# Routing and places of a mixture of experts: one product for all places, reordered rows, plain writes, held weight loads

## The chip, the cores and the metric

The kernel runs on one core of one Trainium2 chip. The metric is the device time of that core in microseconds (us), the median of several runs. Before the change it is 1528.69 us (median of 3 runs, 1525.78 to 1528.85).

## What is computed

Two transformer blocks on 512 tokens of 1024 channels: a recurrent mixer with a feed-forward layer, then a second mixer with a mixture of experts. Only the last part matters here. Shortened:

```python
h2 = rms_norm(x) * g2 * (1 + sc2) + sh2        # 512 rows of 1024
g_idx = argmax(h2 @ w_group + b_group)          # one group of 4 for each token
top_vals, e_idx = top_k(logits of that group's 4 experts, 2)
weights = p_g * softmax(top_vals)
for each of 16 experts:                         # d_expert = 256
    y += (silu(h2 @ gate) * (h2 @ up) * combine) @ down
out = x + gt2 * y
```

Each token goes to two experts, so an expert has 64 tokens on average. The kernel keeps 128 places for each expert and one further slot (number 16) for an expert with more.

## The kernel before, in words

Everything is unrolled. TensorE (PE) multiplies, VectorE (DVE) and ScalarE (ACT) prepare operands and take results out of PSUM, SyncE (SP) issues the plain loads, GpSimd (POOL) issues the DMAs that accumulate, gather or scatter. float32 products are made of three passes on split operands (`hi`, `lo`): ACT copies a weight piece into `hi` (L1279), DVE subtracts it into `lo` (L1280).

The order of the end of the kernel:

- **Last product** (L1282 to L1309). For each of 4 blocks `tb` of 128 tokens, 24 matmuls (L1289 to L1291) give the second half of the output projection. `x2half` (L1253) multiplies by `gt1r`, adds to the rows `x1t` (L1255, L1256) and squares (L1257). Then the block's rows are transposed (L1295), multiplied by the router (L1298), turned back (L1300) and summed into the logits `lg` (L1303 to L1305); the inverse root comes from `rsq1` (L227 to L232). Last, DVE forms the normed row `h` (L1308) and POOL adds it with an accumulating DMA to `d_h2` in DRAM (L1309; the profile calls it `d_h`), which an earlier SP DMA had filled with the shift `sh2`. Here the planner orders the engines' work by priority.
- **Routing** (L1313 to L1339). `largest` (L1315) finds the first and second choice of each token, `abf` marks its two experts, a triangular product (L1336) counts ranks, `cola` is the rank plus one and `col_` the rank.
- **Places.** For an expert, `onehot` (L1342) compares the ranks of all tokens with 0 to 127, giving `O`, and `placed` (L1346) multiplies `O` with `tk` (token number and weight in parts) by 4 matmuls (L1349). `infos` (L1350) takes the token numbers into `idx` and the weights into `wcl` (L1352 to L1355). Expert 0's `idx` is made first and alone (L1451 to L1454), experts 0 to 4 come in `places` (L1356), each later one inside the expert loop, five experts ahead.
- **Gather.** `gather` (L1403) lets POOL fetch the 128 rows of an expert from `d_h2` into `xg` by `idx` (L1405); three buffers. Rows beyond the expert's count are skipped.
- **Expert loop** (from L1477, an order written out by hand for PE, DVE and ACT). An expert's weights are six pieces of 512 KB: 0 to 3 for gate and up, 4 and 5 for down. `up_piece` (L1415 to L1424), `up_end` with the silu (L1426), `act_in` (transposes L1431, copies L1433), `down` (L1436 to L1445) and the scatter, an indirect accumulating DMA into `out` (L1446). PE does expert e+1's first up piece, then e's transposes L1431, then the rest of e+1's up, then e's down. At e=3 to 7 DVE has the steps of `further`, at e=11 those of `extra` (L1383 to L1389), for slot 16.
- **Weight loads.** `wfetch` (L1209) issues a piece on SP (L1215) into the next of 26 slots; a slot is given back when its piece is converted (or, for piece 5, used). Ten pieces (`NR`) are issued before the last branch merge, the others as slots come free. `pieces` (L1394) is the order in which pieces are used, `ensure` converts up to `LA`=3 pieces ahead.

With slot 16 there are 17 experts of 6 pieces, 102 pieces.

## Time and profile before

| | us |
|---|---|
| median of 3 runs | 1528.69 |
| the profiled execution | 1528.76 |
| its span, first to last instruction | 1527.0 |
| PE busy | 1431.6 (94%) |
| DVE busy | 1035.8 (68%) |
| ACT busy | 642.9 (42%) |
| POOL busy | 100.5 (7%) |

The profile has several views. The page gives busy shares, and the span in 40 slices of 38 us, with a digit for the tenths that an engine was busy. Windows give the same for stretches that one chooses, with the granted clock of TensorE as a share of full speed and the share of time in which the 16 DMA engines had packets under way. The timeline lists instructions by their start. The DMA view lists issues with the median time from issue to landing. In the timeline a row is: start, duration, engine, source line, operation, output and inputs, shapes, and in brackets the idle time before it and what ended that.

### The profile page before, as it was taken

Reading aid. Unit: us, or ns where it says so; the run is one execution under the profiler, and the core shown is the slowest. Engines: PE = TensorE matmul, PEld = TensorE weight load, DVE = VectorE, ACT = ScalarE, POOL = GpSimd, SP = SyncE. Lnnn points to the kernel's source line nnn. Section 1 sums busy time; section 2 is a strip of 40 time slices with the busy share of each in tenths; the row PEclk is TensorE's granted clock in tenths of the full one; section 3 lists DMA queues with packets and bytes.
Section 4 is the critical chain, followed back from the end, with each engine's and each line's share of the span. In section 5 each row is a group of like instructions: output and inputs, shape, how many; then the busy total and the mean of one; then the engine's idle time right before and its main releaser. Section 6 shows DMA issues by size and latency. Waiting matters only on the chain. (4 is left out here: it accounts for less than half of the span.)

```text
span 1527.0 us, 23008 instructions
## 1 busy us (share of the span) xinstructions
PE 1431.6 (94%) x8916; PEld 1110.6 (73%) x8916; DVE 1035.8 (68%) x1988; ACT 642.9 (42%) x1042; POOL 100.5 (7%) x116
## 2 busy tenths in 40 slices
PE   7999979899999999899999999999899999399996
PEld 4777857677777787777777777777678887276764
DVE  4887868668787774644649967654543445689994
ACT  5554436233433443323343324463622343265662
POOL 0111100000000000000001000000000000123232
PEclk9999989899999999999999999999899999699998
DMA  5443524052556446554243211122043245889960
GB/s 196 141 142 135 204 65 165 16 177 67 186 198 202 165 141 183 169 203 139 75 151 106 86 62 62 57 99 77 23 179 125 97 149 196 282 295 355 332 219 14
DMA packets 78706, 226.63 MB, mean 148 GB/s; under 512 B 19520, under 2 KB 20160, under 8 KB 78592
## 3 DMA queue, kind: packets, MB, share of 16 engines
q1 hardware_dynamic: 68736, 202.25, 38.4%
...
HBM read 208.52 MB, written 28.07 MB: 155 GB/s over the span
## 5 line engine op out<-in xcount | busy, mean ns | idle before, releaser
L155 DVE TENSOR_TENSOR lo<-raw,hi 128x1024 fp32r<-128x1024 f32 (+1 forms) x183 | 210.7, 1152 | 209.5 <-ACT hi L154 208.4
L154 ACT ACTIVATE hi<-raw 128x1024 fp32r<-128x1024 f32 (+1 forms) x183 | 183.2, 1002 | 389.4 <-PE g L170 223.1
L171 PE MATMUL g<-bh,lo 128*128 128x512 f32 x376 | 152.3, 405 | 2.5 <-DVE lo L155 2.4
L169 PE MATMUL g<-bh,hi 128*128 128x512 f32 x376 | 152.3, 405 | 0.0
L170 PE MATMUL g<-bl,hi 128*128 128x512 f32 x376 | 150.5, 400 | 0.0
L171 PE MATMUL g<-hh,lo 128*128 128x512 f32 x336 | 133.7, 398 | 6.7 <-DVE lo L155 6.7
L169 PE MATMUL g<-hh,hi 128*128 128x512 f32 x336 | 133.7, 398 | 0.0
L170 PE MATMUL g<-hl,hi 128*128 128x512 f32 x336 | 133.2, 397 | 0.0
L171 PEld LDWEIGHTS g<-bh,lo 128*128 128x128 f32 x376 | 71.5, 190 | 22.2 <-DVE lo L155 4.2
L169 PEld LDWEIGHTS g<-bh,hi 128*128 128x128 f32 x376 | 71.8, 191 | 19.1 <-issue 2.0
L170 PEld LDWEIGHTS g<-bl,hi 128*128 128x128 f32 x376 | 71.4, 190 | 16.2 <-issue 0.2
L169 PE MATMUL g<-xh,hi 128*128 128x512 f32 x200 | 80.2, 401 | 0.0
L171 PEld LDWEIGHTS g<-hh,lo 128*128 128x128 f32 x336 | 63.8, 190 | 22.5 <-DVE lo L155 7.6
L861 DVE SCALAR_TENSOR_TENSOR acc<-raw,ca,acc 128x1024 f32<-128x1024 f32 x42 | 53.8, 1282 | 38.7 <-DMA raw<-in_wmod 38.5
L171 PE MATMUL g<-xh,lo 128*128 128x512 f32 x200 | 79.7, 398 | 0.0
L170 PE MATMUL g<-xl,hi 128*128 128x512 f32 x200 | 79.4, 397 | 0.0
L169 PEld LDWEIGHTS g<-hh,hi 128*128 128x128 f32 x336 | 63.9, 190 | 17.9 <-ACT hi L154 3.4
L170 PEld LDWEIGHTS g<-hl,hi 128*128 128x128 f32 x336 | 63.7, 190 | 14.8
L890 DVE SCALAR_TENSOR_TENSOR c<-g,vec,c 128x511 f32<-128x511 f32 x88 | 65.6, 745 | 1.1
L754 PE MATMUL g<-hi,fl 128*128 128x512 f32 x136 | 53.4, 393 | 0.0
L755 PE MATMUL g<-lo,fh 128*128 128x512 f32 x136 | 53.4, 392 | 0.0
L753 PE MATMUL g<-hi,fh 128*128 128x512 f32 x136 | 53.1, 391 | 0.0
...
## 6 DMA issues: line engine op xcount, KB each, us to landing
raw<-in_wexp SPq DMA_DIRECT2D x89, 512.0 KB, 8.4
raw<-in_win SPq DMA_DIRECT2D x74, 512.0 KB, 3.5
raw<-in_wmod SPq DMA_DIRECT2D x48, 512.0 KB, 4.1
raw<-in_wup SPq DMA_DIRECT2D x44, 512.0 KB, 4.1
raw<-in_wdn SPq DMA_DIRECT2D x22, 512.0 KB, 4.0
raw<-in_wout SPq DMA_DIRECT2D x16, 512.0 KB, 4.6
ws<-in_wexp SPq DMA_DIRECT2D x13, 512.0 KB, 10.3
raw<-in_wA SPq DMA_DIRECT2D x12, 512.0 KB, 3.4
```

Of the source, the lines that this page charges most:

```text
L154: S.activation(hi[:,:f],raw[:,:f],AF.Copy)
L155: V.tensor_tensor(lo[:,:f],raw[:,:f],hi.bitcast(F32)[:,:f],op=OP.subtract)
L169: PE.matmul(ps,hi[:,sl],xh[k],start=(k==0),stop=False)
L170: PE.matmul(ps,hi[:,sl],xl[k],start=False,stop=False)
L171: PE.matmul(ps,lo[:,sl],xh[k],start=False,stop=(k==n-1))
L753: PE.matmul(ps,xh[k][:,sl],w[kk][0],start=(k==0),stop=False)
L754: PE.matmul(ps,xl[k][:,sl],w[kk][0],start=False,stop=False)
L755: PE.matmul(ps,xh[k][:,sl],w[kk][1],start=False,stop=(k==2*n-1))
L861: else: V.scalar_tensor_tensor(acc,raw,ca[:,k:k+1],acc,op0=OP.mult,op1=OP.add)
L890: for k in (1,2): V.scalar_tensor_tensor(c[:,k:],ps[:,:512-k],Vc(f'fw{2-k}',i),c[:,k:],op0=OP.mult,op1=OP.add)
```

## The change

Five things are changed. (1) The last product, its logits and the routing get an order written by hand, in which block tb-1's transposes and logits stand between block tb's products. (2) Only blocks 0 and 1 of `d_h2` are filled with the shift and accumulated into; for blocks 2 and 3 the shift is added on DVE and SP writes the rows plainly. (3) The places of all 16 experts are found at once: the rank `rk` of each token's first and second choice gives eight one-hots `Ak` of 128 places, and one product of 8 matmuls gives all 16 columns of `idx`, a second one later all weights; the per-expert `onehot`, `placed` and `infos` go away, except for slot 16. (4) No further weight piece is issued by SP until the first gather has landed: a DMA of 16 numbers that reads the gathered rows (`d_hold`) is put in SP's queue ahead of them. The ten first pieces remain. (5) Expert 15's down product is moved between the second and third up piece of slot 16.

```diff
-    with tc.issue_after(ug_.ins): nc.sync.dma_start(d_h2,bass.AP(tensor=d_mod.tensor,offset=d_mod.offset+3072,ap=[[0,512],[1,1024]]))
-
-    oh=pd2.tile([128,384],F32,name='oh',tag='l'); nc.sync.dma_start(oh,A['oh'])
+
+    oh=pd2.tile([128,384],F32,name='oh',tag='l'); oh_=nc.sync.dma_start(oh,A['oh'])
+    with tc.issue_after(oh_.ins): nc.sync.dma_start(d_h2[0:256,:],bass.AP(tensor=d_mod.tensor,offset=d_mod.offset+3072,ap=[[0,256],[1,1024]]))
...
-    for i in (0,2,3):
+    for i in range(4):
         m=pe_.tile([128,1024],F32,name='modr',tag=f'modr{i}'); modr.append(m)
         nc.sync.dma_start(m,bass.AP(tensor=d_mod.tensor,offset=d_mod.offset+2048+1024*i,ap=[[0,128],[1,1024]]))
-    gt1r,a2r,gt2r=modr
+    gt1r,sh2r,a2r,gt2r=modr
...
+    hold=[None]
     def wnext(whole=False):
         if not AS: AS.extend([act2.tile([128,2,1024],F32 if t_[2]=='1' else FR,name='ws',tag=t_) for t_ in ('Ah0','Al0','Ah1','Al1')])
-        while todo and any(p!='AS' or not todo[0][1] for p,_ in slots): wfetch(*todo.pop(0))
+        if hold[0]:
+            with tc.issue_after(hold[0]) if hold[0]!='done' else ExitStack():
+                while todo and any(p!='AS' or not todo[0][1] for p,_ in slots): wfetch(*todo.pop(0))
+            if len(done)>=3: hold[0]='done'
...
-        x2half(tb,1,ps)
-        nc.scalar.dma_start(out[sl,:],x1t[tb])
...
+    man=ExitStack(); man.enter_context(tc.manual_schedule(engines={ET.PE,ET.DVE,ET.Activation}))
...
-        v=small(3,'nv'); V.tensor_scalar(v[:,0:1],ssq[:,tb,0:1],ssq[:,tb,1:2],1e-6,op0=OP.add,op1=OP.add)
-        rsq1(v[:,0:1],v[:,1:2],v[:,2:3])
...
-        lgi=V.scalar_tensor_tensor(lg[:,tb,:],lg[:,tb,:],v[:,1:2],rbias,op0=OP.mult,op1=OP.add)
-        h=pw.tile([128,1024],F32,name='h2',tag='h2')
-        with tc.issue_after(lgi.ins):
-            V.scalar_tensor_tensor(h,x1t[tb],v[:,1:2],a2r,op0=OP.mult,op1=OP.mult)
-        G.dma_start(d_h2[sl,:],h,accum_op=OP.add)
+        V.scalar_tensor_tensor(lg[:,tb,:],lg[:,tb,:],blk[tb]['v'][:,1:2],rbias,op0=OP.mult,op1=OP.add)
+    def inverse(tb):
+        blk[tb]['v']=v=small(3,'nv'); V.tensor_scalar(v[:,0:1],ssq[:,tb,0:1],ssq[:,tb,1:2],1e-6,op0=OP.add,op1=OP.add)
+        rsq1(v[:,0:1],v[:,1:2],v[:,2:3])
+    def scaled(tb):
+        blk[tb]['h']=h=pw.tile([128,1024],F32,name='h2',tag='h2'); V.tensor_tensor(h,x1t[tb],a2r,op=OP.mult)
+    def rows_out(tb):
+        v=blk[tb]['v'][:,1:2]
+        if tb<2:
+            h=pw.tile([128,1024],F32,name='h2',tag='h2'); V.scalar_tensor_tensor(h,x1t[tb],v,a2r,op0=OP.mult,op1=OP.mult)
+            G.dma_start(d_h2[tb*128:tb*128+128,:],h,accum_op=OP.add)
+        else:
+            h=blk[tb]['h']; V.scalar_tensor_tensor(h,h,v,sh2r,op0=OP.mult,op1=OP.add)
+            nc.sync.dma_start(d_h2[tb*128:tb*128+128,:],h)
+    for tb in range(4):
+        ps=pg.tile([128,512],F32,name='g',tag='g')
+        product(tb,ps,0); product(tb,ps,1)
+        if tb: turned(tb-1)
+        product(tb,ps,2)
+        if tb: logits(tb-1)
+        product(tb,ps,3)
+        if tb: added(tb-1)
+        x2half(tb,1,ps)
+        nc.scalar.dma_start(out[tb*128:tb*128+128,:],x1t[tb])
+        if tb: rows_out(tb-1)
+        inverse(tb)
+        if tb>=2: scaled(tb)
+    turned(3); logits(3); added(3); rows_out(3)
...
-    os_=tt('os',4,4); V.tensor_tensor(os_,o1_,o2_,op=OP.add)
-    abf=pe_.tile([128,4,16],BF,name='abf'); V.tensor_tensor(abf.rearrange('p t (g e) -> p t g e',g=4),os_,g44,op=OP.mult)
+    og=pe_.tile([128,2,4,16],BF,name='og')
+    for k,oh_ in enumerate((oh1,oh2)): V.tensor_tensor(og[:,k].rearrange('p t (g e) -> p t g e',g=4),v4(oh_)[:,:,1:5,:],g44,op=OP.mult)
+    abf=pe_.tile([128,4,16],BF,name='abf'); V.tensor_tensor(abf,og[:,0],og[:,1],op=OP.add)
...
+    og8=og.rearrange('p k t e -> p (k t) e')
+    bt=pe_.tile([128,2,4,2,16],BF,name='bt')
+    for k in range(2): V.tensor_tensor(bt[:,k],og[:,k][:,:,None,:].to_broadcast([128,4,2,16]),tk[:,:,0,0:2][:,:,:,None].to_broadcast([128,4,2,16]),op=OP.mult)
+    ge=tt('ge',4); V.tensor_tensor(ge,lg[:,:,0:4],mx1[:,:,0][:,:,None].to_broadcast([128,4,4]),op=OP.subtract); S.activation(ge,ge,AF.Exp)
     cola=tt('cola',16); V.scalar_tensor_tensor(cola,rps[:,0:64].rearrange('p (t e) -> p t e',t=4),1.0,abf,op0=OP.add,op1=OP.mult)
-    col_=tt('col_',16); V.tensor_scalar(col_,cola,1.0,None,op0=OP.subtract)
-    iota=C3('iota')
+    ck=sq_pool.tile([128,2,4,16],F32,name='ck',tag='sq',bufs=3); V.tensor_tensor(ck,og,cola[:,None].to_broadcast([128,2,4,16]),op=OP.mult)
+    rk=pe_.tile([128,8],F32,name='rk'); V.tensor_reduce(rk,ck.rearrange('p k t e -> p (k t) e'),axis=AX,op=OP.add)
+
+    iota=C3('iota'); iota1=C3('iota1')
+    Ak=pe_.tile([128,8,128],BF,name='Ak')
+    for k in range(2): V.tensor_tensor(Ak[:,4*k:4*k+4],iota1[:,None,:].to_broadcast([128,4,128]),rk[:,4*k:4*k+4][:,:,None].to_broadcast([128,4,128]),op=OP.is_equal)
     idx=pe_.tile([128,17],U32,name='idx'); wcl=pe_.tile([128,17],F32,name='wcl')
+    def at_places(B,n):
+        ps=pt()
+        with order():
+            for i in range(8): PE.matmul(ps[:,:n],Ak[:,i,:],B[:,i,:],start=(i==0),stop=(i==7))
+        return ps
+    ps=at_places(bt.rearrange('p k t c e -> p (k t) (c e)'),32)
+    cnt=pe_.tile([128,16],F32,name='cnt'); V.tensor_copy(cnt,rps[:,64:80])
+    ips=pe_.tile([128,32],F32,name='ips'); V.tensor_copy(ips,ps[:,:32])
+    V.scalar_tensor_tensor(idx[:,0:16],ips[:,0:16],4096.0,ips[:,16:32],op0=OP.add,op1=OP.add)
...
-    def places(e0,e1):
-        ips=pm.tile([128,17,8],F32,name='m',tag='m')
-        for e in range(e0,e1): placed(onehot(col_[:,:,e]),lambda tb:tk[:,tb,e,:],ips,e)
-        infos(ips,e0,e1,wcl,idx)
...
-    pieces+=[(16,4),(16,5)]
+    pieces[-6:]=[(16,0),(16,1),(15,4),(15,5),(16,2),(16,3),(16,4),(16,5)]
...
-    O=onehot(col_[:,:,0]); ips=pm.tile([128,17,8],F32,name='m',tag='m')
-    with order():
-        for i in range(8): PE.matmul(ips[:,0,0:1],O[:,i//2,:],tk[:,i//2,0,i%2:i%2+1],start=(i==0),stop=(i==7))
-    idx0=pe_.tile([128,1],U32,name='idx0'); V.tensor_scalar(idx0,ips[:,0,0:1],4096.0,None,op0=OP.add)
-    xgs=[gather(idx0)]; ensure(2)
-
-    b4=lambda t_: t_[:,:,None].to_broadcast([128,4,4])
-    b44=lambda t_: t_[:,:,None,None].to_broadcast([128,4,4,4])
-    ge=tt('ge',4); V.tensor_tensor(ge,lg[:,:,0:4],b4(mx1[:,:,0]),op=OP.subtract); S.activation(ge,ge,AF.Exp)
+    xgs=[gather(idx[:,i:i+1]) for i in range(3)]
+
+    d_hold=dten('d_hold',[1,16]); hold[0]=nc.sync.dma_start(d_hold,xgs[0][0:1,0:16]).ins
+    ensure(1)
...
+    xin=rows_in(xgs[0],0); ps=psum()
...
-    places(0,5); xgs.append(gather(idx[:,1:2]))
+        V.tensor_copy(wp[:,p],m12)
+        if p<2: V.tensor_tensor(m12,m12,wp[:,p],op=OP.subtract)
+    bw=pe_.tile([128,8,3,16],BF,name='bw')
+    for p in range(3): V.tensor_tensor(bw[:,:,p,:],og8,wp[:,p].rearrange('p k t -> p (k t)')[:,:,None].to_broadcast([128,8,16]),op=OP.mult)
+    for p in range(4):
+        up_piece(ps,xin,p,piece(0,p))
+        if p==1: wps=at_places(bw.rearrange('p i c e -> p i (c e)'),48)
+    wpc=pe_.tile([128,48],F32,name='wpc'); V.tensor_copy(wpc,wps[:,:48])
+    V.tensor_tensor(wcl[:,0:16],wpc[:,0:16],wpc[:,16:32],op=OP.add); V.tensor_tensor(wcl[:,0:16],wcl[:,0:16],wpc[:,32:48],op=OP.add)
+    a=up_end(ps,wcl[:,0:1])
+    xin=rows_in(xgs[1],1); xgs.append(gather(idx[:,3:4]))
+    for p in range(3): V.tensor_tensor(tk[:,:,:,2+p],bw[:,0:4,p,:],bw[:,4:8,p,:],op=OP.add)
...
+    for e in range(17):
+        O=None
+        if e<13: xgs.append(gather(idx[:,e+4:e+5]))
+        if e==3: fur=further()
+        if 3<=e<8: next(fur,None)
+        if e==11: xps=pm.tile([128,17,8],F32,name='m',tag='m'); O=extra(0,xps,16)
+        if e==8:
+            e0=nc.values_load(ei[0:1,0:1],min_val=0,max_val=15,engines=[ET.SP])
+            w0=[(A['wexp'][bass.ds(e0,1),p].rearrange('o p f -> (o p) f'),p==5) for p in range(6)]
+            todo+=w0[:2]+wx(15,(4,5))+w0[2:]
+        if e<16: ps=psum(); up_piece(ps,xin,0,piece(e+1,0))
+        aa=act_in(a)
+        if e<16:
+            for p in range(1,4):
+                if e==15 and p==2: down(aa,piece(e,4),piece(e,5),idx[:,e:e+1])
+                up_piece(ps,xin,p,piece(e+1,p))
+            a=up_end(ps,wcl[:,e+1:e+2])
+        if O: placed(*O)
+        if e<15: xin=rows_in(xgs[e+2],e+2)
+        if e!=15: down(aa,piece(e,4),piece(e,5),idx[:,e:e+1])
+        if O: infos(xps,16,17,wcl,idx)
...
-            if s_<16: ips=pm.tile([128,17,8],F32,name='m',tag='m'); O=(onehot(col_[:,:,s_]),lambda tb:tk[:,tb,s_,:],ips,s_)
...
-            if O: infos(ips,s_,s_+1,wcl,idx)
```

## Rows read from the trace of the kernel before

**Rows 1.** The page: PE's busy tenths in 40 slices of the span.

```profile
PE   7999979899999999899999999999899999399996
```

**Rows 2.** Windows: length, PE, PEld, DVE, ACT, POOL busy, PE clock, DMA share, GB/s.

```profile
1310.00:1320.00 10.00, 2.05 (x31) 1.13 (x31) 7.47 (x25) 0.28 (x1) 0.84 (x1) 0.50 1.03 321
1324.00:1328.00 4.00, 0.00 (x0) 0.00 (x0) 3.69 (x15) 0.00 (x0) 1.60 (x1) 0.50 1.02 418
1350.00:1375.00 25.00, 25.00 (x124) 18.53 (x124) 23.66 (x37) 17.61 (x26) 5.25 (x4) 1.00 0.94 311
1425.00:1450.00 25.00, 25.00 (x118) 18.36 (x117) 24.77 (x43) 17.22 (x27) 6.24 (x4) 1.00 1.01 334
1475.00:1500.00 25.00, 25.00 (x114) 18.75 (x113) 23.02 (x29) 17.62 (x26) 5.67 (x3) 1.00 0.13 26
```

**Rows 3.** Timeline from the last product's end to expert 0's list of rows.

```profile
1305.42 0.40 PE L1291 MATMUL g<-lo,gh 128*128 128x512 f32 x1
...
1307.80 0.69 DVE L1256 TENSOR_TENSOR x1t<-x1t,g 128x512 f32<-128x512 f32 x1
...
1311.63 0.24 DVE L1303 TENSOR_REDUCE l<-m 128x20 f32<-128x80 f32 x1 [0.86 <-PE m L1300]
...
1312.28 1.28 DVE L1308 SCALAR_TENSOR_TENSOR h<-x1t,nv,modr 128x1024 f32<-128x1024 f32 x1
1313.47 0.23 DVE L1316 TENSOR_REDUCE mx<-lg 128x20 f32<-128x80 f32 x1
...
1317.72 0.69 DVE L1344 TENSOR_TENSOR O<-cst,col__11733 128x512 bf16<-128x512 f32 x1
...
1318.89 0.16 DVE L1454 TENSOR_SCALAR idx<-m 128x1 uint32<-128x1 f32 x1 [0.48 <-PE m L1453]
```

**Rows 4.** Timeline: the first gather, and PE's first use of it.

```profile
1323.73 1.87 POOL L1405 DMA_INDIRECT xg<-d_h,idx  x1 [9.03 <-ACT ws L1279]
...
1332.23 0.66 PE L1411 MATMUL m<-cst,xg 128*128 128x128 f32 x2 [3.86 <-DMA xg<-d_h,idx]
```

**Rows 5.** DMA, us to landing: last block's write (1313.86), gathers 1, 2, plain DRAM writes.

```profile
d_h<-h POOLq DMA_DIRECT2D x1, 512.0 KB, 8.9
xg<-d_h,idx POOLq DMA_INDIRECT x1, 8.4
xg<-d_h,idx POOLq DMA_INDIRECT x1, 5.8
d_x<-xr SPq DMA_DIRECT2D x4, 512.0 KB, 2.7
```

**Rows 6.** Timeline: transposes L1431, once for each expert (0, 3, 11, 12, 15).

```profile
1345.67 0.38 PE L1431 MATMUL m<-cst,a 128*128 128x128 f32 x2
...
1375.41 0.38 PE L1431 MATMUL m<-cst,a 128*128 128x128 f32 x2
...
1458.65 0.38 PE L1431 MATMUL m<-cst,a 128*128 128x128 f32 x2
...
1471.27 0.38 PE L1431 MATMUL m<-cst,a 128*128 128x128 f32 x2
...
1500.52 0.38 PE L1431 MATMUL m<-cst,a 128*128 128x128 f32 x2
```

**Rows 7.** DMA, weight pieces issued before 1190, in 1350 to 1375, 1450 to 1475.

```profile
raw<-in_wexp SPq DMA_DIRECT2D x10, 512.0 KB, 5.0
...
raw<-in_wexp SPq DMA_DIRECT2D x13, 512.0 KB, 6.6
...
raw<-in_wexp SPq DMA_DIRECT2D x9, 512.0 KB, 13.7
```

**Rows 8.** Timeline: slot 16's transposes, its last result, its scatter.

```profile
1508.03 0.38 PE L1431 MATMUL m<-cst,a 128*128 128x128 f32 x2
...
1512.45 0.69 DVE L1445 TENSOR_TENSOR ye<-g,modr 128x512 f32<-128x512 f32 x1 [0.86 <-PE g L1444]
...
1515.88 1.54 POOL L1446 DMA_INDIRECT out<-ye,idx  x1 [5.15 <-DMA out<-ye,idx]
```

More of the change, by code (lines that the diff above doesn't have):

```diff
@@ L1294, in build, with product, turned @@
+    blk=[{} for _ in range(4)]
+    def product(tb,ps,p):
+        sl=slice(tb*128,tb*128+128); hi,lo=wl1[p]
+        for kk in range(2):
+            k=2*p+kk; c=slice(kk*512,kk*512+512)
+            PE.matmul(ps,mh[k][:,sl],hi[:,c],start=(k==0),stop=False)
+            PE.matmul(ps,ml[k][:,sl],hi[:,c],start=False,stop=False)
+            PE.matmul(ps,mh[k][:,sl],lo[:,c],start=False,stop=(k==7))
+    def turned(tb):
         ps=pt((128,4,128))
         for k in range(4): PE.transpose(ps[:,k,:],x1t[tb][:,(4+k)*128:(4+k)*128+128],ident)
-        hc=pw.tile([128,4,128],F32,name='hc',tag='hc'); S.activation(hc,ps,AF.Copy)
+        blk[tb]['hc']=hc=pw.tile([128,4,128],F32,name='hc',tag='hc'); S.activation(hc,ps,AF.Copy)
```

75 lines of the change are left out of this document (20 added, 55 removed).

## The prediction, made before the change was run

> **What bounds the kernel now.** I read the page first: PE is busy in nearly every slice, with one dip near the end, at digit 35 of 40 [rows 1]. A slice is 38 us, so the dip lies near 1310. All edits but one small write lie from there on. The windows, read second, show a hole: from 1310 to 1320 PE works 2 of 10 us at a granted clock of 0.50, which is the level of 1.2 GHz, while the DMA engines have packets under way all the time; from 1324 to 1328 PE does nothing and DMA moves 418 GB/s [rows 2]. The timeline tells who is waited for. The last product ends at 1305.8, its rows are complete at 1308.5, the logits bring the routing to 1313.5, expert 0's list is there at 1319.05 [rows 3]. But its gather starts only at 1323.7 and PE only at 1332.2 [rows 4]: the last block's accumulating write, issued at 1313.86, took 8.9 us and landed at 1322.8, and then the gather took 8.4 us [rows 5].
>
> Behind the hole the loop runs with three engines near their limits: from 1425 to 1450 DVE is busy 24.8 of 25 us and the DMA share is 1.01 [rows 2]. L1431 comes once for each expert, so its spacing is the period: (1375.41-1345.67)/3 = 9.91 us, (1458.65-1375.41)/8 = 10.41 while DVE also has the steps of `further`, 12.62 with `extra`, and (1500.52-1471.27)/3 = 9.75 at the end [rows 6], where DVE has fallen to 23.0 of 25 and loads are over [rows 2]. 9.75 is what PE alone needs. The loads are a bound that hides: a piece issued between 1350 and 1375 lands after 6.6 us, one between 1450 and 1475 after 13.7 [rows 7]. The queue grows, so supply is slower than use, and only the lead built up in the hole carries the loop.
>
> **Part by part.**
> *Start of the routing.* In the new order `added(2)` stands ahead of `x2half(3)` on DVE, about 0.6 us, but the planner's former insertion of `h` between L1255 and L1256 (1.28 us as L1308 [rows 3]) goes, so rows are complete some 0.3 us earlier. Then DVE has `rows_out(2)` (1.28), `inverse(3)` (about 1.5, seven small operations) and `scaled(3)` (1.28, like L1308) before the logits' sum, which was reached 3.1 us after the rows [rows 3]; the three end after 3.9. Net +0.4: L1316 at 1313.9. A wait is added here: `scaled(3)` needs the buffer of block 1's row, free when its accumulating DMA lands. That is issued near 1301.8 and I give it the 8.9 us of its kind [rows 5], so 1310.7, just as DVE gets there; a later landing would delay the logits queued behind it on DVE one for one.
>
> *Places.* One more small operation (0.25), two small products and `ge` while PE counts ranks (0.2 not hidden), `ck` and `rk` in place of `col_` (+0.35), a second one-hot operation of 0.69 that starts 0.63 after the first, and one copy (0.2): +1.65 on a path that took 1313.47 to 1319.05 [rows 3]. All lists at 1319.05+0.4+1.65 = 1321.1.
>
> *Rows written plainly.* `rows_out(3)` ends at 1313.9 and SP has nothing else due, so the write is issued then. Plain DRAM writes of this size land after 2.7 us [rows 5], at 1316.6; even 4 us more would be hidden by the places. The gather then waits for the list and starts at 1321.4 rather than 1323.7.
>
> *Gather, loads held.* Its latency was 8.4 us among loads and 5.8 for the second gather, issued while loads were few [rows 5]. With none at all I take 5.0, below the nearest row as its queue is emptier still; ends 4 and 8.4. It lands at 1326.4 instead of 1332.1, 5.7 us sooner. Two more gathers follow on POOL at once; they are needed 9 us later, which hides them. The wait that the change adds is SP's: `d_hold` waits for this landing with all further pieces behind it. Ten pieces are there [rows 7]: enough for expert 0 and expert 1's up product, some 15 us of PE.
>
> The Trainium skill, "DMA: Bandwidth & Descriptors", section "Queues, rings and completion order", says that a DMA engine takes its queues in turn, packet by packet. By that a gather of 0.25 MB gets half the rate whatever stands in the weight queue, and holding loads would win only about 0.6 us. The rows speak against it: 8.4 with loads, 5.8 with few.
>
> *First expert.* L1411 to L1431 took 13.44 us [rows 4, 6], half of it at the low clock. The 20 matmuls of the first lists go, the 8 of the weights come (0.4 us): I leave it. First L1431 at 1326.5+13.4 = 1339.9, 5.8 earlier than 1345.67.
>
> *Loop.* DVE loses `O` (0.69 [rows 3]) and four operations of about 0.16 for each of 11 experts, some 1.1 us of a period, so `further` fits where it stretched the period to 10.41; PE loses 4 small matmuls. I take 14 periods at 9.75 and 11.9 for the one with `extra` (between 9.75 and 12.62, near the upper end, since `extra` stays whole): 148.4 against 154.85. L1431 of expert 15 comes at 1488.3, if weights are there.
>
> *End.* From L1431 of expert 15 to the last scatter it was 15.36 us [rows 6, 8]. The last result was ready at 1513.14 but the scatter waited for the one before, to 1515.88 [rows 8]. With expert 15's down product 2.8 us earlier that wait goes (-2.6); PE, though, now waits for slot 16's silu and copies with nothing else to do (+0.75). 13.5 us: last scatter at 1501.8. From there to the end of the span it is 1527.0-1515.9 = 11.1, unchanged.
>
> **Two lines for the end.** PE's line: 1501.8+11.1 = 1512.9. The supply line: 92 of 102 pieces must come after the hold is lifted at 1326.4. In the 4 us window of nearly pure loads, 418 GB/s, 512 KB take 1.25 us [rows 2]. In the loop latency grew by 7.1 us in 100 [rows 7], so supply needs 10.41 x 1.071 = 11.15 us for what one expert uses: six pieces (7.5) and a gather with a scatter (3.65, or 1.83 each). After the hold there are 92 x 1.25 = 115 us of pieces and, before the last one lands, 16 gathers and 14 scatters, 55 us: 170. With 1 us for the first to arrive, the last piece lands at 1497.4; slot 16's last up piece, third from the end, at 1494.9. After it come the conversions on ACT and DVE (about 2.4, as 128x1024 operations [rows 3]), six matmuls (1.4), silu and scaling (1.2), and from L1431 to the last scatter 1508.03 to 1513.14 and 0.2 [rows 8]: 10.3. Last scatter 1505.2, end 1516.3. The later line decides: the supply. The profiled execution was 1528.76 with a span of 1527.0, 1.8 outside it; so 1518. It stands 0.07 above the median of the runs, which changes nothing.
>
> In short: the hole is 5.7 us shorter, the loop would win 6.4 and the end 1.9, 14 in all; holding the loads gives back 3.4 at the end, as some 19 pieces that came during the hole now come behind it.
>
> **Rivals.**
> A. *Supply keeps up, PE sets the end*: 1512.9+1.8 = 1514.7. For it: the windows hold 334 GB/s with PE at its own pace [rows 2]; if gathers and scatters cost less when fewer wait, the 3.4 go. Against: the growing latency [rows 7]. The Trainium skill, "DMA: Bandwidth & Descriptors", section "Specifications", gives about 358 GB/s of HBM bandwidth for a core. By it 92 pieces (48.2 MB) and 30 transfers of 0.25 MB take 155 us, the stream ends near 1483 and this rival is the result. The trace shows 418 in one window and 311 to 334 in others at shares of 0.94 and 1.01 [rows 2], so I see no such ceiling in either direction.
> B. *The gather lands no sooner* although the queue is empty (8.4 us; the latency is then POOL's and the scattered rows'): start and hold shift by 3.4 us, and so does the supply line: 1521.5. This is also where the round-robin rule leads.
> C. *Slower: the stream starves the loop.* The forecast needs 55.7 MB in 170 us, 328 GB/s. From 1350 to 1375, with gathers and scatters, it was 311 [rows 2]: then 179 us and 1527. Before's time is met at 309 GB/s; at 300, not far below that row, it is 186 us and 1534. Nothing loaded ahead is left to cover it. Against: that window had a share of 0.94 and so some idle queue.
> D. *The change doesn't do what it says*: loads stay ahead of `d_hold` on SP, or DVE's new order stalls at `scaled(3)`; then the start moves by 2 us or less either way and the end by the loop's gain alone: 1520 to 1526.
>
> **How the numbers follow.** Forecast (supply-bound, 1516 to 1520) 0.48; A 0.2; B 0.12; C 0.12; D 0.08. Likeliest: 1518. Low end: A with a gather of 4 us, `extra` hidden and a better end, 1508. High end: C at its row, and a little, 1528. Outside lies about 2 in 10, most of it in C. A measurement of this kernel tells 0.2% (3 us) from no change: faster is below 1525.6, slower above 1531.7. Forecast, A, B and half of D are faster, with a little of C: 0.82. Same takes the rest of D and the middle of C: 0.09. Slower: 0.09.
>
> **What would show it.** Right: PE's gap from L1291's end to the first L1411 near 20.7 us instead of 26.4; the first gather's latency near 5; L1431 spaced 9.75 in the first eight experts; then PE waiting for `lo` or `ws` (L1280), and behind that for weights from DMA, in the last five; the DMA share at 1.0 until about 1497; the last scatter not waiting for the one before. Wrong: a gather above 7 us; no DMA wait in the late loop (A); such waits from expert 4 on (C); L1316 after 1315 (`scaled(3)` stalls); DVE, not DMA, ending PE's waits.

## The result, and the profile after

The changed kernel takes 1508.62 us (median of 4 runs, 1507.33 to 1510.62) against 1528.57 for the kernel before in the same comparison: ratio 0.987, 95% interval 0.9854 to 0.9887. The forecast was 1518, in the range 1508 to 1528. The profiled execution has a span of 1507.4 us, 19.6 less than before.

Four marks split the span: the end of the last `x1t` (L1256 before, L1257 after), the first transposes of an expert (L1431, now L1470), those of expert 15, and the end. All times in us:

| stretch | before | after | difference | forecast |
|---|---|---|---|---|
| start to the last `x1t` | 1308.49 | 1300.30 | -8.19 | -0.3 |
| to the first transposes of an expert | 37.18 | 31.13 | -6.05 | -5.5 |
| to those of expert 15 | 154.85 | 151.07 | -3.78 | -6.4 |
| to the end of the span | 26.46 | 24.88 | -1.58 | -1.9, and +3.4 for the supply |
| span | 1526.98 | 1507.38 | -19.60 | -10.7 |

The largest part lies where I had not looked. Before the change, windows (length, PE busy, granted clock, DMA share, GB/s) show a hole of some 5 us near 612, half way through the kernel:

```profile
605.00:610.00 5.00, 4.73 (x21) 1.00 0.75 280
610.00:615.00 5.00, 0.00 (x0) 0.84 0.33 127
615.00:620.00 5.00, 4.23 (x10) 0.50 0.63 211
```

The DMA issues of 593 to 602 (KB, median us from issue to landing), the waits of 585 to 625 (us, times, longest) and two rows of the timeline of the kernel before name the cause. The fill of `d_h2` (2 MB) was issued at 593.50 and three weight pieces stood behind it on SP's queue; they took 11.5 to 14.6 us. VectorE stood from 600.93 to 610.64 at L861, for the first piece of `in_wmod`. PE waited for a `lo` of another piece, whose `hi` was ready at 604.55 (L154, 1.06 us from 603.49): it stood behind L861 in VectorE's order and came at 614.50.

```profile
d_h<-d_mod SPq DMA_DIRECT2D x1, 2048.0 KB, 13.9
raw<-in_wmod SPq DMA_DIRECT2D x2, 512.0 KB, 12.5
raw<-in_wup SPq DMA_DIRECT2D x1, 512.0 KB, 14.6
...
DVE acc L861 <- DMA raw<-in_wmod: 10.7, 3, 9.7
...
PE g L171 <- DVE lo L155: 6.0, 1, 6.0
...
610.64 1.28 DVE L861 SCALAR_TENSOR_TENSOR acc<-raw,ca,acc 128x1024 f32<-128x1024 f32 x1 [9.71 <-DMA raw<-in_wmod]
...
614.50 1.22 DVE L155 TENSOR_TENSOR lo<-raw,hi 128x1024 fp32r<-128x1024 f32 x1
```

PE lost more than the 6.0 us of this wait: behind it the granted clock was 0.50 until about 620, and matmuls came 0.42 us apart instead of 0.23. After, the fill (1 MB) is issued at 802.66 and the hole is gone:

```profile
605.00:610.00 5.00, 5.00 (x23) 1.00 0.73 249
610.00:615.00 5.00, 5.00 (x24) 1.00 0.50 154
615.00:620.00 5.00, 5.00 (x23) 1.00 0.65 206
```

The windows after that answer to [rows 2] (columns as there). The expert loop begins at 398 and 366 GB/s, where [rows 2] had 311. Over more windows the difference is smaller: the mean is 354 GB/s from 1325 to 1475, and before it was 333 from 1350 to 1475. PE is busy without a gap from 1350 to 1425 and again from 1450; around the period with `extra` it is not. The stream of weights is over by about 1476:

```profile
1313.00:1318.00 5.00, 0.00 (x0) 0.00 (x0) 3.75 (x9) 2.10 (x3) 3.66 (x3) 0.50 0.44 136
1325.00:1350.00 25.00, 23.86 (x110) 17.91 (x109) 22.09 (x32) 18.12 (x27) 5.34 (x4) 1.00 1.03 398
1350.00:1375.00 25.00, 25.00 (x114) 19.13 (x113) 23.96 (x35) 15.89 (x25) 6.54 (x4) 1.00 1.03 366
1425.00:1450.00 25.00, 23.14 (x101) 17.20 (x99) 23.10 (x34) 15.80 (x24) 6.79 (x5) 0.93 0.97 319
```

The start of the routing, the list, the first gather and PE's first use of it, answering [rows 3, 4]:

```profile
1299.61 0.69 DVE L1257 TENSOR_TENSOR x1t<-x1t,g 128x512 f32<-128x512 f32 x1
...
1305.78 0.23 DVE L1342 TENSOR_REDUCE mx<-lg 128x20 f32<-128x80 f32 x1
...
1312.33 0.17 DVE L1385 SCALAR_TENSOR_TENSOR idx<-ips 128x16 uint32<-128x16 f32 x1
...
1313.46 1.17 POOL L1444 DMA_INDIRECT xg<-d_h,idx  x1 [17.48 <-DVE idx L1385]
...
1318.04 0.87 PE L1450 MATMUL m<-cst,xg 128*128 128x128 f32 x3 [5.97 <-DMA xg<-d_h,idx]
```

The transposes L1470 of experts 0, 11, 12 and 15, answering [rows 6]: periods are (1439.44-1331.43)/11 = 9.82, then 13.63 with `extra`, then 9.81.

```profile
1331.43 0.38 PE L1470 MATMUL m<-cst,a 128*128 128x128 f32 x2
...
1439.44 0.38 PE L1470 MATMUL m<-cst,a 128*128 128x128 f32 x2
...
1453.07 0.38 PE L1470 MATMUL m<-cst,a 128*128 128x128 f32 x2
...
1482.50 0.38 PE L1470 MATMUL m<-cst,a 128*128 128x128 f32 x2
```

PE's waits from 1331 to 1492 add up to 3.3 us, and none of them is for weights from DMA:

```profile
PE g L1463 <- DVE ws L1285: 1.9, 1, 1.9
PE m L1470 <- DVE a L1466: 1.0, 1, 1.0
PE g L1480 <- ACT ah L1472: 0.4, 1, 0.4
```

### The profile page after: what moved, and what is told of

Read it like the earlier page. It is cut to its first block, busy times and chain, and to the rows that moved or that the text cites. A ratio compares the mean times of both kernels' runs of the same rounds, so it can differ in the third digit from the quotient of the medians.

```text
span 1507.4 us, 22836 instructions
## 1 busy us (share of the span) xinstructions
PE 1426.6 (95%) x8860; PEld 1110.1 (74%) x8860; DVE 1026.8 (68%) x1937; ACT 643.3 (43%) x1042; POOL 95.8 (6%) x114
```

## The experiments

The part of the kernel ahead of the last `x1t` is the same, or nearly, in all kernels whose fill is late, and yet it ended between 1298.51 and 1302.98 in them. So beside the time I give the stretches of the table above, from the profiled execution of each.

| kernel | time, median | last `x1t` | to first transposes | to expert 15 | to the end | `x1t` to end |
|---|---|---|---|---|---|---|
| before | 1528.57 | 1308.49 | 37.18 | 154.85 | 26.46 | 218.49 |
| after | 1508.62 | 1300.30 | 31.13 | 151.07 | 24.88 | 207.08 |
| e1_fill_late | 1523.79 | 1300.56 | 37.58 | 156.51 | 26.39 | 220.48 |
| e2_fill_early | 1518.29 | 1308.57 | 31.30 | 151.14 | 25.41 | 207.85 |
| e3_no_hold | 1512.81 | 1299.17 | 34.58 | 151.08 | 25.48 | 211.13 |
| e4_accumulated | 1509.72 | 1301.88 | 31.22 | 151.08 | 25.37 | 207.68 |
| e5_spread | 1509.33 | 1302.14 | 30.80 | 147.43 | 28.43 | 206.67 |
| e6_old_end | 1509.21 | 1299.25 | 31.53 | 151.13 | 26.14 | 208.79 |
| e7_hold_third | 1508.17 | 1300.98 | 31.16 | 151.07 | 25.51 | 207.74 |
| e8_onehots_back | 1515.21 | 1298.51 | 30.83 | 155.01 | 25.22 | 211.07 |
| e9_pool | 1513.33 | 1302.98 | 32.26 | 149.51 | 27.35 | 209.12 |
| e11_spread_early | 1505.87 | 1301.89 | 30.88 | 147.43 | 24.71 | 203.01 |
| e12_best | 1506.00 | 1299.91 | 31.03 | 147.43 | 26.58 | 205.04 |
| e13_spread_two | 1513.95 | 1308.94 | 31.49 | 147.43 | 24.95 | 203.86 |

The kernel before had medians of 1531.43 beside e1 to e4, 1531.74 beside e5 to e8, 1530.97 beside e9, e11 and e13, and 1532.90 beside e12. It moved by up to 4.3 us between these groups, so medians are best compared within a group.

**e1: the fill alone, in the kernel before.**

```diff
-    with tc.issue_after(ug_.ins): nc.sync.dma_start(d_h2,bass.AP(tensor=d_mod.tensor,offset=d_mod.offset+3072,ap=[[0,512],[1,1024]]))
-    oh=pd2.tile([128,384],F32,name='oh',tag='l'); nc.sync.dma_start(oh,A['oh'])
+    oh=pd2.tile([128,384],F32,name='oh',tag='l'); oh_=nc.sync.dma_start(oh,A['oh'])
+    with tc.issue_after(oh_.ins): nc.sync.dma_start(d_h2,bass.AP(tensor=d_mod.tensor,offset=d_mod.offset+3072,ap=[[0,512],[1,1024]]))
```

> The kernel before, with one edit: the fill of d_h2 (all 512 rows, 2 MB) is issued behind the load of oh instead of behind the last product of u. Theory: before, the fill was issued on SP at 593.50 ahead of three weight loads, which then took 14.6, 13.4 and 11.5 us and left PE idle from 610 to 615; moved, this gap goes, every later instruction lies about 8.2 us earlier, and the span is about 1518.8, the time about 1520.5 us. Rival: the fill's 2 MB only stand in the way of other transfers at their new place, and PE loses the same elsewhere; then the time stays at 1528.6 us, and the 20 us of the change come from its routing and its expert loop alone.

Ratio to before 0.9953 (0.9937 to 0.9968), 7.6 us by the medians; the last `x1t` lies 7.9 us earlier, and PE works through the hole:

```profile
610.00:615.00 5.00, 5.00 (x23) 1.00 0.59 204
```

The pieces behind the old place of the fill now land in 4.3 to 4.5 us. Two microseconds were lost again behind the last `x1t`, mostly in the `extra` period (14.24 for 12.62). PE's wait in it is 2.4 us in both kernels, but here the granted clock was 0.50 behind it (1459 to 1461), and in the kernel before it stayed at 1.00.

**e2: the fill back at its old place, in the changed kernel.**

```diff
-    oh=pd2.tile([128,384],F32,name='oh',tag='l'); oh_=nc.sync.dma_start(oh,A['oh'])
-    with tc.issue_after(oh_.ins): nc.sync.dma_start(d_h2[0:256,:],bass.AP(tensor=d_mod.tensor,offset=d_mod.offset+3072,ap=[[0,256],[1,1024]]))
+    with tc.issue_after(ug_.ins): nc.sync.dma_start(d_h2,bass.AP(tensor=d_mod.tensor,offset=d_mod.offset+3072,ap=[[0,512],[1,1024]]))
+    oh=pd2.tile([128,384],F32,name='oh',tag='l'); nc.sync.dma_start(oh,A['oh'])
```

> The changed kernel, with the fill of d_h2 back at its old place and in its old size (512 rows, behind the last product of u). All other edits stay. Theory: the gap at 610 to 615 is back, about 8.2 us; the time is about 1516.8 us, and the other edits together are worth about 12 us. Rival (the fill's place is worth nothing): 1508.6 us.

1518.29, 9.7 above the changed kernel by the medians, and 8.6 above e4 (below), which was timed beside it and differs little from the changed kernel; in the trace the last `x1t` is back at 1308.57 (+8.27) and the rest within 0.8 us of after. The hole is back as well:

```profile
605.00:610.00 5.00, 2.37 (x11) 1.00 0.43 174
610.00:615.00 5.00, 0.95 (x2) 0.65 0.55 145
```

Both ways round the fill's place is worth about 8 us. It is the same 8 us in either kernel, so it does not depend on the routing or the loop. Nor does it need the smaller fill: e1 moves all 2 MB.

**e3: no hold.**

```diff
-        if hold[0]:
-            with tc.issue_after(hold[0]) if hold[0]!='done' else ExitStack():
-                while todo and any(p!='AS' or not todo[0][1] for p,_ in slots): wfetch(*todo.pop(0))
-            if len(done)>=3: hold[0]='done'
+        while todo and any(p!='AS' or not todo[0][1] for p,_ in slots): wfetch(*todo.pop(0))
...
-    d_hold=dten('d_hold',[1,16]); hold[0]=nc.sync.dma_start(d_hold,xgs[0][0:1,0:16]).ins
```

> The changed kernel without the hold: the expert weights are fetched as soon as their buffers are free, in SP's order, and d_hold is not written. Theory: the first gather again shares the DMA engines with the weight stream and takes 8 to 8.5 us instead of 4.45, so the first transposes of xg come 3.5 to 4 us later and the time is about 1512.3 us; the earlier stream gives nothing back, since PE sets the loop. Rival: the gather's latency does not depend on the stream; then the first transposes stay, and the time is 1508.6 us or, with the weights there sooner, up to 1 us below.

1512.81, 3.1 above e4, and the first transposes of `xg` 21.22 us behind the last `x1t` instead of 17.74. The first gather, us to landing, without the hold:

```profile
xg<-d_h,idx POOLq DMA_INDIRECT x1, 7.7
```

and with it (the changed kernel):

```profile
xg<-d_h,idx POOLq DMA_INDIRECT x1, 4.4
```

So the latency hangs on what else the DMA engines have, and holding the weights is worth 3.5 us at the start. The 16 pieces that were issued ahead of the gather here gave nothing back in the loop (151.08).

**e4: accumulating writes kept.**

```diff
-    with tc.issue_after(oh_.ins): nc.sync.dma_start(d_h2[0:256,:],bass.AP(tensor=d_mod.tensor,offset=d_mod.offset+3072,ap=[[0,256],[1,1024]]))
+    with tc.issue_after(oh_.ins): nc.sync.dma_start(d_h2,bass.AP(tensor=d_mod.tensor,offset=d_mod.offset+3072,ap=[[0,512],[1,1024]]))
...
-            h=blk[tb]['h']; V.scalar_tensor_tensor(h,h,v,sh2r,op0=OP.mult,op1=OP.add)
-            nc.sync.dma_start(d_h2[tb*128:tb*128+128,:],h)
+            h=blk[tb]['h']; V.scalar_tensor_tensor(h,x1t[tb],v,a2r,op0=OP.mult,op1=OP.mult)
+            G.dma_start(d_h2[tb*128:tb*128+128,:],h,accum_op=OP.add)
```

> The changed kernel, but blocks 2 and 3 of the rows are added onto the fill by POOL as in the kernel before (the fill at its new place with all 512 rows), with DVE's two steps for each block kept. Theory: with the weights held back the accumulating write of block 3, issued at about 1306, lands in 5 to 6 us, at 1311 to 1312, before the index at 1312.5; so the plain writes are worth nothing by themselves and the time is 1508.6 us, within 1. Rival: the accumulating write takes 8.9 us as in the kernel before; it lands at about 1315, the first gather starts about 1.5 to 2.5 us later, and the time is 1510.1 to 1511.1 us.

1509.72, and 207.68 from `x1t` to the end against 207.08. The last block's accumulating write landed 5.1 us after its issue at 1307.75, ahead of the list of rows, where [rows 5] has 8.9 among the loads:

```profile
d_h<-h POOLq DMA_DIRECT2D x1, 512.0 KB, 5.1
```

With the weights held back, then, the plain writes are worth nothing that can be told. Without the hold they had a use: in e3 the gather starts 0.94 us behind the list; in the kernel before it waited for the accumulating write and started 4.68 behind.

**e7: the hold on the third gather.**

```diff
-    d_hold=dten('d_hold',[1,16]); hold[0]=nc.sync.dma_start(d_hold,xgs[0][0:1,0:16]).ins
+    d_hold=dten('d_hold',[1,16]); hold[0]=nc.sync.dma_start(d_hold,xgs[2][0:1,0:16]).ins
```

> The changed kernel, with the weights held until the third gather has landed instead of the first: the stream of weights starts some 6 us later, and PE's first use of a gathered row does not move. Theory (PE sets the loop, the stream has slack): periods stay 9.8, up to 2 us are lost at the extra expert, 1508.6 to 1510.6 us. Rival (the supply line of the forecast, a stream that just keeps up and sets the end): all 6 us come out at the end, 1514.5 us.

The weights start 21.4 us behind the last `x1t` instead of 18.0, 3.4 later and not 6, since the third gather was quicker without them. All periods stay (151.07) and the time is 1508.17. The supply does not set the end of the changed kernel; its slack is at least these 3.4 us.

**e8: the one-hots back in the loop.**

```diff
+        if e<11: dps=pm.tile([128,17,8],F32,name='m',tag='m'); O=(onehot(cola[:,:,e+5]),lambda tb:tk[:,tb,e+5,:],dps,e+5)
...
-        if O: infos(xps,16,17,wcl,idx)
+        if O: infos(*((xps,16,17,wcl,idx) if e==11 else (dps,e+5,e+6,wcl,idx)))
```

> The changed kernel, with the one-hot, the product of four and the read-out of experts 5 to 15 put back into periods 0 to 10, as in the kernel before (they give the same indices and weights again). Theory (the loop gained from VectorE's relief, and from four products less on PE): periods go to about 9.9, and to 10.7 where further() runs (experts 4 to 7), as before, 5 us more: about 1513.6 us. Rival (the loop gained from the held stream of weights or from their new slots): periods stay 9.82, 1508.6 us.

1515.21 (1511.79 to 1518.16; the profiled execution is the first of these, the fastest). Periods are 9.95 to 9.97, 10.73 to 10.78 where `further` runs and 12.60 with `extra`, and the loop takes 155.01 us: what it took before. A stretch as long as a period with `further` shows VectorE nearly full and PE waiting (columns as in [rows 2]):

```profile
1379.97:1390.77 10.80, 10.29 (x50) 7.39 (x49) 10.70 (x19) 6.64 (x10) 3.14 (x2) 1.00 0.96 357
```

In the changed kernel, over the length of its own period, PE is full and VectorE just inside:

```profile
1379.97:1389.79 9.82, 9.82 (x46) 7.39 (x45) 9.67 (x14) 6.65 (x10) 3.35 (x2) 1.00 1.01 359
```

So the loop's gain is not the stream's. Where `further` runs it is VectorE's relief, 0.9 us of a period. In the other periods of e8 PE is full too (10.00 of 10.00 us from 1421.4 to 1431.4), and the 0.14 us by which they are longer go with the four small products that e8 gives back to PE.

**e6: the old end.**

```diff
-    pieces[-6:]=[(16,0),(16,1),(15,4),(15,5),(16,2),(16,3),(16,4),(16,5)]
+    pieces+=[(16,4),(16,5)]
...
-            todo+=w0[:2]+wx(15,(4,5))+w0[2:]
+            todo+=w0[:4]+wx(15,(4,5))+w0[4:]
...
-                if e==15 and p==2: down(aa,piece(e,4),piece(e,5),idx[:,e:e+1])
...
-        if e!=15: down(aa,piece(e,4),piece(e,5),idx[:,e:e+1])
+        down(aa,piece(e,4),piece(e,5),idx[:,e:e+1])
```

> The changed kernel, with the end as in the kernel before: the last pieces in their old order, and the down product of expert 15 behind the whole up product of expert 16. Theory (the end was a step of its own): about 1.0 to 1.9 us slower, 1509.6 to 1510.5 us. Rival: the last scatter waits for the landing of the one before it in either order, and nothing is lost: 1508.6 us.

26.14 us from expert 15's transposes to the end against 24.88; 1.26 us for this part in the trace, which the medians (1509.21) are too coarse to tell. The last scatter again waits 2.8 us for the one before, as in [rows 8].

**e5: the extra expert's steps spread.** In the long period `extra`'s steps stand on VectorE ahead of the split that PE waits for (timeline of the changed kernel):

```profile
1441.14 1.09 DVE L1426 TENSOR_TENSOR tx<-tk,eq 128x512 f32<-128x512 bf16 x1
...
1443.67 1.22 DVE L1285 TENSOR_TENSOR ws<-raw,ws 128x1024 fp32r<-128x1024 f32 x1
...
1444.95 0.50 PE L1463 MATMUL g<-ws,xgh 128*128 128x512 f32 x1 [1.86 <-DVE ws L1285]
```

The wait of 1.86 us is not all of it. In e9, below, whose loop is the same, PE waits 1.87 us at this place, and the period takes 12.07 us instead of 13.63. The 5 us behind the wait, in the changed kernel and in e9, differ in the granted clock (PE busy, clock, DMA share, GB/s):

```profile
1445.00:1450.00 5.00, 5.00 (x22) 0.66 0.94 296
...
1449.00:1454.00 5.00, 5.00 (x27) 1.00 0.94 295
```

So 1.6 us of this period are TensorE's clock. Why it fell here and not in e9 stays open. The edit of e5 takes the wait away:

```diff
+        yield
...
+        yield
...
-        return onehot(cc),lambda tb:tb_[:,tb,:],ps,s
+        yield
+        yield onehot(cc),lambda tb:tb_[:,tb,:],ps,s
...
-        if e==11: xps=pm.tile([128,17,8],F32,name='m',tag='m'); O=extra(0,xps,16)
+        if e==8: ex=extra(0,None,16)
+        if 8<=e<11: next(ex)
+        if e==11: xps=pm.tile([128,17,8],F32,name='m',tag='m'); O=next(ex); O=(O[0],O[1],xps,16)
...
-        for j in range(1,7): placed(*extra(j,xps,j))
+        for j in range(1,7): placed(*list(extra(j,xps,j))[-1])
```

> The changed kernel, with VectorE's steps for the seventeenth (extra) expert spread over experts 8 to 11 instead of all in expert 11. Theory: in the changed kernel that one period takes 13.63 us instead of 9.82 because VectorE's 3.5 us of these steps stand ahead of the splits that PE waits for; spread, they fit beside PE as the five steps of further() do, all periods are 9.8 to 9.9 and the time is about 1505.0 us. Rival: the period is long because a piece of weights lands late there (ScalarE waited 1.2 us for a DMA at 1442.47); then the period stays above 12.5 and the time is 1508 to 1509 us.

Right about the period (9.96 instead of 13.63) and wrong about the time (1509.33; e7, timed beside it, has 1508.17). The loop is 3.6 us shorter and the end 3.6 us longer. POOL's scatters show where it went:

```profile
1475.27 1.54 POOL L1487 DMA_INDIRECT out<-ye,idx  x1 [6.93 <-DMA out<-ye,idx]
1483.55 2.44 POOL L1487 DMA_INDIRECT out<-ye,idx  x1 [6.75 <-DVE ws L1285]
1491.41 1.54 POOL L1487 DMA_INDIRECT out<-ye,idx  x1 [5.42 <-DMA out<-ye,idx]
1498.01 1.54 POOL L1487 DMA_INDIRECT out<-ye,idx  x1 [5.05 <-DMA out<-ye,idx]
```

The `y` of these four were ready 3.7, 1.9, 4.5 and 2.1 us before. TensorE's clock fell here too (0.66 from 1490 to 1495) and made the last `y` 1.6 us later, but even so it had to wait. A scatter adds to `out` and waits until the one before has landed. While the stream runs that takes some 9 us (9.04 for the one that e11, below, issues at 1436.31) and 0.8 from that landing to the next start at 1446.15, 9.84 in all: just PE's period. The scatters are a line of their own, as long as PE's; whoever shortened only PE's, here, got nothing.

**e13: the spread, and two lines of scatters** (the edit against e5; what goes to the scratch array is left out of the output).

```diff
-    d_h2=dr.tile([512,1024],F32,name='d_h2')
+    d_h2=dr.tile([512,1024],F32,name='d_h2'); d_s2=dr.tile([512,1024],F32,name='d_s2'); nsc=[0]
...
+    nc.sync.dma_start(d_s2,bass.AP(tensor=d_mod.tensor,offset=d_mod.offset+3072,ap=[[0,512],[1,1024]]))
...
-        G.indirect_dma_start(out=out,out_offset=bass.IndirectOffsetOnAxis(ap=ix,axis=0),in_=y,in_offset=None,
+        nsc[0]+=1
+        G.indirect_dma_start(out=out if nsc[0]%2 else d_s2,out_offset=bass.IndirectOffsetOnAxis(ap=ix,axis=0),in_=y,in_offset=None,
```

> The kernel with the extra expert's steps spread, and in addition every second scatter goes to a scratch array instead of the output (their sum into the output is left out), so that a scatter waits for the one two before it, not for the one before. The scratch array is filled behind d_h2's fill. Theory (the line of scatters took the spread kernel's gain): no scatter starts later than 0.5 us behind its y, and from the transposes of expert 15 to the last scatter it takes about 14.4 us instead of 17.6; the time is about 1505.0 us. Rival (something else of the spread kernel's end is late, as TensorE's clock, which fell to 0.66 there): the end stays as it was, 1508.6 to 1509.3 us.

Every scatter shown starts 0.28 us behind its `y`, the last one 14.14 us behind the transposes of expert 15 (17.63 in the kernel with the spread alone):

```profile
1489.13 1.54 POOL L1489 DMA_INDIRECT out<-ye,idx  x1 [6.54 <-DVE al L1476]
1494.66 1.54 POOL L1489 DMA_INDIRECT d_s<-ye,idx  x1 [3.99 <-DVE ye L1487]
1501.99 1.54 POOL L1489 DMA_INDIRECT out<-ye,idx  x1 [5.78 <-DVE ye L1487]
```

From `x1t` to the end it is 203.86, 2.8 less than the spread alone. The time, 1513.95, went the other way for a reason that I had not meant: without an order given, the planner put the fill of the scratch array (2 MB) at 593.12, the old place of `d_h2`'s, and the hole came back with it, last `x1t` 1308.94:

```profile
610.00:615.00 5.00, 0.00 (x0) 0.70 0.34 114
```

**e11: the spread, and six pieces ahead of the hold** (against e5).

```diff
+            for _ in range(4 if tb==2 else 2): wfetch(*todo.pop(0))
```

> The kernel with the extra expert's steps spread (its loop took 3.7 us less, and its end gave them all back: scatter 14 waited for scatter 13's landing, 15 for 14's and 16 for 15's), and in addition six of the held pieces of weights fetched ahead of the hold, four behind block 2's rows and two behind block 3's, where the DMA engines stood idle. Theory: the scatters form a line of their own, each waiting for the landing of the one before, about 9 us while the stream runs and 5 to 6 behind it; a stream that ends 6 to 7 us earlier frees the line, the last scatter starts within 1 us of its y, and the time is about 1505.0 us. Rival: the scatters' latency does not hang on the stream, or the six pieces delay the first gather by as much: 1508.6 to 1510 us.

1505.87, and 203.01 from `x1t` to the end, 4.1 less than the changed kernel. The first transposes of `xg` come 17.78 us behind `x1t` (17.74), so the pieces cost the gather nothing; the scatters have caught up before the last one, which starts 0.3 us behind its `y`. The stream is over sooner: the DMA share is 0.12 from 1470 to 1475, where the spread alone has 0.97.

**e9: block 3's rows off VectorE.**

```diff
-        blk[tb]['h']=h=pw.tile([128,1024],F32,name='h2',tag='h2'); V.tensor_tensor(h,x1t[tb],a2r,op=OP.mult)
+        blk[tb]['h']=h=pw.tile([128,1024],F32,name='h2',tag='h2'); (G if tb==3 else V).tensor_tensor(h,x1t[tb],a2r,op=OP.mult)
...
-            h=blk[tb]['h']; V.scalar_tensor_tensor(h,h,v,sh2r,op0=OP.mult,op1=OP.add)
+            h=blk[tb]['h']
+            if tb==3: S.activation(h,h,AF.Copy,scale=v); G.tensor_tensor(h,h,sh2r,op=OP.add)
+            else: V.scalar_tensor_tensor(h,h,v,sh2r,op0=OP.mult,op1=OP.add)
...
+        if tb==3: scaled(tb)
...
-        if tb>=2: scaled(tb)
+        if tb==2: scaled(tb)
```

> The changed kernel, with the scaling of block 3's rows (1.22 us) and their last step (1.28 us) taken off VectorE: POOL multiplies by a2r, ScalarE by the inverse norm, POOL adds sh2r. Theory: from 1301.4 to 1312.5 VectorE has no gap, so it alone sets the time of the first index; 2.0 to 2.5 us less on it bring the first gather to about 11.0 us behind the last x1t instead of 13.16, and the time to about 1506.5 us. Rival: POOL's two steps on 128x1024 are long (the longest of POOL's own in the trace, a fill of 128x1024, took 1.03 us; a product of two tiles is not in the trace), block 3's write lands behind the index and the gather waits for it: 1508.6 to 1511 us.

Slower, 1513.33, and 1.5 us later at the first transposes of `xg`, by neither way that I had named. Block 3's write was not what was late: the list itself was, at 13.6 us behind `x1t` instead of 12.2. VectorE stood still while POOL worked (timeline):

```profile
1303.18 3.20 POOL L1313 TENSOR_TENSOR h<-x1t,modr 128x1024 f32<-128x1024 f32 x1 [4.52 <-DMA d_h<-h]
...
1304.52 1.87 DVE L229 SCALAR_TENSOR_TENSOR nv<-nv 128x1 f32<-128x1 f32 x1
...
1308.54 2.37 POOL L1321 TENSOR_TENSOR h<-h,modr 128x1024 f32<-128x1024 f32 x1 [2.16 <-ACT h L1321]
1308.81 2.20 DVE L1349 SCALAR_TENSOR_TENSOR oh<-pre,eqs 128x80 f32<-128x80 f32 x1
```

L229 takes 0.22 and L1349 0.24 us otherwise; both end with POOL's product (1303.18+3.20 = 1306.38, 1304.52+1.87 = 1306.39). The loop is 1.6 us shorter by its `extra` period, as said at e5, and the end 2.5 longer: the last scatter waits 2.8 us for the one before, as in e5.

**e12: e11, and a shorter way to the first gather** (against e11).

```diff
+    def half3():
+        blk[3]['q']=q=sq_pool.tile([128,512],F32,name='q',tag='sq',bufs=3); V.tensor_tensor(q,x1t[3][:,0:512],a2r[:,0:512],op=OP.mult)
...
+        if tb==3:
+            blk[3]['h']=h=pw.tile([128,1024],F32,name='h2',tag='h2'); V.tensor_tensor(h[:,512:],x1t[3][:,512:],a2r[:,512:],op=OP.mult); return
...
-            h=blk[tb]['h']; V.scalar_tensor_tensor(h,h,v,sh2r,op0=OP.mult,op1=OP.add)
+            h=blk[tb]['h']
+            for c in ([slice(0,1024)] if tb==2 else [slice(0,512),slice(512,1024)]):
+                V.scalar_tensor_tensor(h[:,c],blk[3]['q'] if tb==3 and c.start==0 else h[:,c],v,sh2r[:,c],op0=OP.mult,op1=OP.add)
...
+        if tb==2: half3()
...
-    ensure(1)
...
-    chosen('m1',mx1); chosen('m2',mx2)
+    chosen('m1',mx1); chosen('m2',mx2); ensure(1)
```

> The changed kernel with the spread of the extra expert's steps and the six early pieces, and two edits more on the way to the first index and gather: the left half of block 3's rows is scaled ahead of its last product, where VectorE waited 0.89 us, and the first split of an expert weight on VectorE (1.22 us) stands behind four small steps instead of right behind the index. Theory: the half takes 0.6 us from VectorE's line, so the first gather of xg lies about 12.55 us behind the last x1t instead of 13.16; and if the split of 1.22 us that runs as the gather would start (1312.43 to 1313.65) is what makes POOL start 0.96 us behind the index, where scatters start 0.28 us behind their y, the gather starts 0.3 us behind the index and lies at 11.9. Time: 1504.0 us, or 1504.6 if only the half counts; the changed kernel alone took 1508.6. Rival: the 0.96 us is POOL's own preparation for a list of indices that it has just got, and stays; and the end stays bound by the scatters, so that nothing comes out behind the 1505.9 us of the kernel with the spread and the six pieces.

1506.00, nothing beyond e11. The list came 0.37 us sooner behind `x1t`, and POOL still started the gather 0.96 us behind it, with the split of 1.22 us moved back to 1312.24:

```profile
1311.57 0.17 DVE L1393 SCALAR_TENSOR_TENSOR idx<-ips 128x16 uint32<-128x16 f32 x1
...
1312.24 1.22 DVE L1285 TENSOR_TENSOR lo<-raw,hi 128x1024 fp32r<-128x1024 f32 x1
1312.70 1.73 POOL L1454 DMA_INDIRECT xg<-d_h,idx  x1 [17.11 <-DVE m L1503]
```

So that split is not what makes the 0.96. The gather then took 5.1 us, and PE used it 18.0 us behind `x1t` (17.8 in e11). At the end PE's granted clock was 0.90 from 1485 to 1490 and 0.76 from 1490 to 1495, where e11 had 1.00 with the same 3.64 of 5 us busy in the first of them; 1.6 us more from expert 15's transposes to the last `y`. Why it fell in the one and not in the other stays open. Both medians lie some 2.7 us below the changed kernel's, but the three were not timed side by side; by their ratios to the kernel before, e11 has 0.9833 (0.9816 to 0.9849) and e12 0.9825 (0.9809 to 0.9841), against 0.987 (0.9854 to 0.9887).

## Why the prediction was right in its direction, and 9.4 us high

- **The step that was missed: "All edits but one small write lie from there on."** I called the fill of `d_h2` a small write and gave it no price. The five points of the change do not name its move either; only the diff does, from behind the last product of `u` to behind the load of `oh`. What moved was 2 MB on SP's queue with three weight pieces queued behind it, a VectorE that stood waiting for one of them, and PE's next operand behind that: 8 us, two fifths of the result (e1, e2, and e13 unasked). The window that shows it, PE busy 0.00 of 5 us from 610 to 615, is one digit 8 among the 9s in [rows 1], where a slice is 38 us. Without these 8.19 us the profiled time would have been 1509.3+8.2 = 1517.5, by the forecast's 1518; that is partly luck, see below. And that 1508.62 still lies inside the range, 0.6 us from its low end, is luck as well: the fill's 8 us are in none of the gains from which that end was worked out.
- *Start of the routing*: 5.48 us from `x1t` to `largest` against 4.98; +0.5, forecast +0.4 on a start 0.3 earlier, so +0.7. `scaled(3)` did not stall. Right.
- *Places*: 5.58 us from `largest` to the list became 6.72, +1.14; forecast +1.65. Too dear by 0.5. (From `x1t` to the list 10.56 became 12.20, +1.64, where start and places together had +2.35.)
- *Plain write, hidden*: right, and e4 shows that even an accumulating one would have been.
- *Gather, loads held*: 4.45 us where I took 5.0; e3 shows the mechanism (7.7 without the hold). POOL started 0.96 us behind the list where I had 0.3, which cancels what start and places came out cheaper: the gather starts 13.16 us behind `x1t`, forecast 13.2. So the 0.55 us by which it lands sooner remain, and the first expert's transposes came 6.05 us sooner, forecast 5.5 in this stretch. The rule of the Trainium skill, "DMA: Bandwidth & Descriptors", section "Queues, rings and completion order", that engines take queues in turn, would by the prediction's estimate have made the hold worth 0.6 us; e3 measures 3.5.
- *First expert*: 13.44 us became 13.39, taken as 13.4. Right; but about 5 us of it lie at the low clock, not half (the granted clock is 1.00 again by 1338 before and by 1324 after).
- *Loop*: the reason was right (e8), two sizes were not. The period is 9.82 and not 9.75 (1 us over 14 periods), with PE full and the same matmuls in it; why is open. The one with `extra` is 13.63 and not 11.9 (1.7 us). PE's wait in it was sized about right, since e9, with the same wait, has 12.07; what the sum lacks is the clock that fell behind it, 1.6 us. e5, which spreads `extra`'s steps, takes both away (9.96).
- *End*: -1.58 for -1.9, out of errors that nearly cancel. The term "that wait goes (-2.6)" was a little too hopeful: the wait fell from 2.74 to 0.50 us, and the last scatter still starts just behind the landing of the one before (1496.08). PE's part, priced +0.75, cost 1.24: the last `y` is ready 13.86 us behind expert 15's transposes and was ready 12.62 behind. From the last scatter to the end it is 10.5 us and not 11.1. The scatters of the changed kernel:

```profile
1483.65 1.54 POOL L1485 DMA_INDIRECT out<-ye,idx  x1 [7.33 <-DVE ye L1484]
1490.36 1.54 POOL L1485 DMA_INDIRECT out<-ye,idx  x1 [5.17 <-DMA out<-ye,idx]
1496.86 1.54 POOL L1485 DMA_INDIRECT out<-ye,idx  x1 [4.96 <-DVE ye L1484]
```

- *The supply line, "the later line decides: the supply"*: this fell, and rival A took its place. I priced 1.25 us a piece and 1.83 a gather or scatter, 170 us; the stream ran from 1318.3 to about 1476, 158 us. With 1.25 for a piece that leaves 1.4 for a gather or scatter. The price of 1.83 came from a growing latency in the kernel before, read as a rate that would stay; after the change the stream moved 354 GB/s in the mean where before had 333, and why it moved more is not shown. That it was no bound is: e7 starts it 3.4 us later and nothing moves. Rival A was given 0.2; with the loop's two sizes put right its 1514.7 becomes 1517.4, and with the fill's 8.2 it is the result. Its rule from the Trainium skill (the same page, section "Specifications", about 358 GB/s for a core) gave the stream an end near 1483 and so led to the right rival, though the window of 25 us at 398 GB/s is above that figure.

Without the fill the forecast would come out near only because two errors cancel: 3.4 us for a supply that was no bound, and 2.7 us too few for the loop.
